# A tuned two-layer decoder kernel: a new time estimate in the builder's scheduler, and the order of steps that follows from it

## The chip, the cores and the metric

The kernel runs as one program on one core of one Trainium2 chip. The metric is device time in microseconds (us), the median of the runs shown. A core has a matrix engine (PE, with its weight loads as PEld), VectorE (DVE), ScalarE (ACT), GpSimd (POOL) and SyncE (SP, which only issues transfers here). Each engine runs its own list of instructions strictly in the order in which the program wrote them; semaphores make an instruction wait for results of other engines.

## The reference

Two layers over 512 tokens of width 1024, all in float32:

```
h = rms_norm(x);  proj = h @ w_in                 # q,k,v of branches A, B, C and three gates, 5376 columns
yA = MoBA attention (4 heads of 64, blocks of 256)
yB = sliding window 128, 8 query heads on 2 kv heads, with learned sinks
yC = differential attention (two softmax maps, P1 - lambda*P2), per-head norm
x  = x + (sum over b of sigmoid(gate_b) * (y_b @ w_p_b)) @ w_out
u  = causal_conv3(rms_norm(x) @ w_up);  x = x + (silu(u_gate) * u_val) @ w_down
```

q and k of every branch are RMS-normed and rotated before the scores.

## The kernel before

**Number format.** Each float32 operand is split in two parts, `whi`/`wlo` for weights and `H[0]`/`H[1]` for activations: the high part by a copy on ACT, the low part by a subtraction. A product is three matmuls (high·high, high·low, low·high). For a weight tile (128 rows x 1024) `w_prep` (L639) copies on ACT and subtracts either on DVE in one instruction or on POOL in four pieces of 256 columns. It takes POOL where `threads[1:] and est.clock["POOL"] <= est.clock["PE"] + POOL_LEAD`, that is while other work than the dense blocks is at hand; in blocks marked busy it always takes DVE.

**Dense blocks.** `dense` (L703) runs through a fixed list of blocks: per layer the steps of `ORDER` (layer 0) or `ORDER1` (layer 1), then two halves of `w_out`, eleven of `w_up`, two of `w_down`. A step `QC` is the q,k columns of branch C (512 columns, four weight tiles) and its v columns (256 columns, two tiles); `gC0` is half 0 of the gate of C (four tiles); `pC0` is half 0 of its output projection. A block walks its weight tiles; in each tile four output chunks get their matmuls, so that all four chunks end in the last tile. With `major=m` the last m tiles are taken chunk by chunk instead, and the chunks end further apart. Each chunk has a PSUM bank of four, which its evacuation frees.

**Norm ahead of the gates.** The steps before the first gate in an order are "raw": they use x times the gain without 1/rms, and the evacuation multiplies by 1/rms per token. From the first gate on, `H` must be normed. `renorm` (L583) does that for each of the eight 128-channel chunks k, once the last raw block is done with the chunk (`prog`): a multiplication on DVE, a copy on ACT, a subtraction on DVE. A later block's tile may start only when its chunks are in `normed`. Before the change the raw steps are QC and QA, and QA comes v first, then q,k.

**Attention.** `attention` starts when C's q,k block is done. Generators (threads) write its pieces: `prep` rotates and splits q and k for four token tiles (DVE, ACT, then PE transposes with PSUM copies in `move`), `score_thread` the scores, `soft` the masked maximum, exponentials and scaling, `trans_thread` the transposes of P, `spread` their split, `value_thread` the products with v, `gather` the output. The order is C, A, B, each in two halves.

**The planner.** The loop at the end of `trunk` chooses, while the program is built, which thread writes its next instructions. It keeps a simulated clock per engine in `Estimate` (L174): `cost` prices an instruction by engine, operation and size, `note` advances the clocks and records when a result is there, `ready` asks when a tensor can be read. A PE thread is taken if its inputs are ready by the PE clock plus `TOL`; otherwise the earliest. Threads of other engines are taken by priority (the `P_...` numbers and `RENORM`, smaller first) if they fit before that limit. The engines then execute this fixed order. So a wrong price puts a PE instruction ahead of data that is not there, and everything behind it on PE waits.

In `Estimate` before, a result is there 0.16 us (`SEM`) after its engine is free, for every engine and also for the same engine; a tensor's time is one number for all its pieces; DVE and POOL instructions that both read SBUF twice, or read it on POOL, wait for each other in the model.

Of the kernel before, what the change touches and what calls it, by code (L numbers as in the profile page):

```python
# [59 lines left out]
MAJ_OUT = 3  # L60
MAJ_DOWN = 0
MAJ_LAST = 3
FINE = 1
SPILL = 8

# [106 lines left out]


class Estimate:  # L174
    SEM = 0.16

    def __init__(self):
        self.clock = {"PE": 0.0, "ACT": 0.0, "DVE": 0.0, "POOL": 0.0, "SP": 0.3, "DGE": 0.0, "DMA": 0.0}
        self.table = None
        self.mode = None  # L180
        self.written = {}
        self.used = {}
        self.pred = {}
        self.rings = {}
        self.lock = LOCK
        self.port = {"DVE": deque(maxlen=24), "POOL": deque(maxlen=24)}

    def alloc(self, tag, bufs, t):
# [8 lines left out]
        i = len(ring) - bufs + n - 1  # L197
        return self.used.get(ring[i], 0.0) if i >= 0 else 0.0

    def ready(self, t):  # L200
        return self.written.get(t.tensor.name, 0.0) + self.SEM

    def cost(self, key, op, out, ins, kw, args):
        n = out.free_size()
        psum = any(x.space == bass.MemoryType.PSUM for x in (out, *ins))
        if key == "PE":
            move = op == "transpose"
            half = (out if move else ins[0]).dtype != F32
            was, self.mode = self.mode, (move, half)
            if move:  # L210
                return 0.072 if half else 0.109
            n = ins[1].free_size()
            if not half:
                return 2 * max(0.111, 8.4e-4 * n)
            return (0.0 if was in (None, self.mode) else 0.075) + max(0.111, 0.0133 + n / 2400)
        if key == "ACT":
            c = (0.053 if psum else 0.114) + 8.3e-4 * max([n] + [x.free_size() for x in ins])
# [9 lines left out]
            return c + (0.093 if "accum_out" in kw else 0.0)  # L227
        n = max([n] + [x.free_size() for x in ins])
        if key == "POOL":
            if kw.get("op") == OP.pow:  # L230
                return 0.3 + 0.165 * n
            return 0.172 + 2.03e-3 * n
        if op == "reciprocal":
            return 0.06 + 7.3e-3 * n
        if op in ("tensor_copy", "tensor_scalar", "memset") and not psum:
            return 0.065 + 6.0e-4 * n
        return (0.13 if op == "scalar_tensor_tensor" else 0.07) + 1.04e-3 * n

    def note(self, key, op, args, kw):
        aps = [x for x in list(args) + list(kw.values()) if isinstance(x, bass.AP)]  # L240
        out = kw.get("out", args[0] if args else None)
        if not isinstance(out, bass.AP):
            return
        outs = [out]
        if "accum_out" in kw and kw["accum_out"] is not None:
            outs.append(kw["accum_out"])
        if op == "tensor_tensor_reduce":
            outs.append(args[-1])
        ins = [x for x in aps if not any(x is o for o in outs)]
        t = self.clock[key]  # L250
        for x in ins:
            t = max(t, self.written.get(x.tensor.name, 0.0) + self.SEM)
        for o in outs:
            nm = o.tensor.name
            if key != "PE" and op != "dma_start":
                t = max(t, self.written.get(nm, 0.0) + (self.SEM if nm in self.written else 0.0))
            if nm[:2] in ("h0", "h1"):
                t = max(t, self.used.get(nm, 0.0) + self.SEM)
            if nm in self.pred:
                t = max(t, self.used.get(self.pred.pop(nm), 0.0) + self.SEM)  # L260
        if op == "dma_start":
            self.clock[key] = t + 0.06
            go = max(t + 0.1, self.clock["DGE"])
            self.clock["DGE"] = go + (0.475 if key == "SP" else 0.66)
            self.clock["DMA"] = max(self.clock["DMA"], go + 1.1) + 1.456 * out.size() / 131072
            end = self.clock["DMA"] + 0.75
        else:
            two = False
            if self.lock and key in ("DVE", "POOL"):
# [6 lines left out]
            if two:  # L276
                for s, e in self.port["POOL" if key == "DVE" else "DVE"]:
                    if s <= t < e:
                        t = e
            end = t + self.cost(key, op, out, ins, kw, args)  # L280
            self.clock[key] = end
            if two:
                gap = 0.05 if key == "POOL" else 0.0
                self.port[key].append((t + gap, end - gap))
        self.last = (t, end)
        for x in ins + outs:
            nm = x.tensor.name
            self.used[nm] = max(self.used.get(nm, 0.0), end)
        for o in outs:
            self.written[o.tensor.name] = max(self.written.get(o.tensor.name, 0.0), end)  # L290


class Thread:
# [37 lines left out]
def trunk(ctx: ExitStack, tc: tile.TileContext, out: bass.AP, a: dict):  # L331
    core = tc.nc
    est = Estimate()
# [1215 lines left out]
    def ready(y):  # L1549
        eng, needs, _ = y  # L1550
        r = 0.0
        for x in needs:
            if callable(x):
                x = x()
            r = max(r, x.when() if isinstance(x, Bufs) else est.alloc_ready(*x) if isinstance(x, tuple) else est.ready(x))
        return r

    def eng_clock(eng):
# [98 lines left out]
```

## Time and profile before

| | us |
|---|---|
| median of 3 runs | 1584.15 (1583.69 to 1584.84) |
| profiled execution, its own time | 1583.99 |
| its span, first to last instruction | 1582.1 |
| PE busy, PEld busy | 1544.0, 1281.9 |
| DVE, ACT, POOL busy | 1048.0, 800.8, 338.9 |

By time the span has these stretches: layer 0's QKV, gates, attention and projections from 0 to about 365, its `w_out` to 430, its `w_up` and `w_down` to about 794; layer 1's in the same order to about 1135, 1208 and the end. The granted PE clock is 0.999 of the upper level. A matmul's busy time covers its whole passage through the array, in which the next one has begun, so PE busy counts some waiting as work.

### The profile page before, as it was taken

Reading aid. Unit: us, or ns where it says so; the run is one execution under the profiler, and the core shown is the slowest. Engines: PE = TensorE matmul, PEld = TensorE weight load, DVE = VectorE, ACT = ScalarE, POOL = GpSimd, SP = SyncE. Lnnn points to the kernel's source line nnn. Section 1 sums busy time; section 2 is a strip of 40 time slices with the busy share of each in tenths; the row PEclk is TensorE's granted clock in tenths of the full one; section 3 lists DMA queues with packets and bytes.
Section 4 is the critical chain, followed back from the end, with each engine's and each line's share of the span. In section 5 each row is a group of like instructions: output and inputs, shape, how many; then the busy total and the mean of one; then the engine's idle time right before and its main releaser. Section 6 shows DMA issues by size and latency. Waiting matters only on the chain.

```text
span 1582.1 us, 21228 instructions
## 1 busy us (share of the span) xinstructions
PE 1544.0 (98%) x7584; PEld 1281.9 (81%) x7584; DVE 1048.0 (66%) x2211; ACT 800.8 (51%) x1566; POOL 338.9 (21%) x455
## 2 busy tenths in 40 slices
PE   8999999999999999999999999999999999999999
PEld 6977888877878888888888787888888788888887
DVE  4798878887576665543249887887776855665231
ACT  7566686764444444333146666766734544444210
POOL 3465443431010000000034564443300200000000
PEclk9999999999999999999999999999999999999999
DMA  5522523214223333333332224322242233223331
GB/s 176 154 68 79 173 68 94 80 54 135 90 83 107 89 98 107 107 98 127 95 114 69 66 79 160 107 67 61 73 159 88 72 106 107 80 86 101 120 120 53
DMA packets 115496, 157.22 MB, mean 99 GB/s; under 512 B 18880, under 2 KB 71104, under 8 KB 115392
## 3 DMA queue, kind: packets, MB, share of 16 engines
q1 hardware_dynamic: 102768, 153.19, 31.3%
q10 hardware_dynamic: 12624, 2.69, 0.9%
q8 instruction: 60, 0.98, 0.3%
q14 instruction: 44, 0.36, 0.1%
HBM read 144.84 MB, written 11.01 MB: 99 GB/s over the span
## 4 chain that ended last, share of the span: by engine, by line
PE 77%; DVE 14%; ACT 4%; DMA 2%; POOL 2%; issue 1%; SPq 0%; ACTq 0%; DVEq 0%; POOLq 0%
PE d L168 70%; PE tp L168 6%; DVE slot L168 5%; DVE temp L168 4%; ACT slot L168 2%; PE s L168 1%; DVE h L168 1%; ACT whi L168 1%; DVE s L168 1%; DMA raw<-in_w_up 1%; DVE wlo L168 1%; POOL rr L168 1%; DVE nb L168 1%; DMA slot<-in_c_cs 0%; ACT h L168 0%
## 5 line engine op out<-in xcount | busy, mean ns | idle before, releaser
L168 PE MATMUL d<-h,whi 128*128 128x512 f32 x2176 | 681.2, 394 | 4.0 <-DVE temp L168 2.7
L168 PEld LDWEIGHTS d<-h,whi 128*128 128x128 f32 x2176 | 398.6, 188 | 84.5 <-ACT temp L168 5.4
L168 PE MATMUL d<-h,wlo 128*128 128x512 f32 x1088 | 424.8, 390 | 0.0
L168 ACT CAST whi<-raw 128x1024 fp32r<-128x1024 f32 x246 | 256.2, 1052 | 280.2 <-PE d L168 136.3
L168 DVE TENSOR_TENSOR wlo<-raw,whi 128x1024 fp32r<-128x1024 f32 x175 | 213.5, 1233 | 257.9 <-ACT whi L168 257.5
L168 POOL TENSOR_TENSOR wlo<-raw,whi 128x256 fp32r<-128x256 f32 x284 | 225.2, 823 | 351.9 <-ACT whi L168 315.2
L168 PE MATMUL d<-slot,whi 128*128 128x512 f32 x864 | 267.0, 390 | 0.0
L168 PEld LDWEIGHTS d<-h,wlo 128*128 128x128 f32 x1088 | 204.2, 188 | 44.0
L168 PE MATMUL d<-whi,h 128*128 128x512 f32 (+1 forms) x768 | 205.9, 346 | 0.6 <-ACT h L168 0.6
L168 PEld LDWEIGHTS d<-slot,whi 128*128 128x128 f32 x864 | 161.1, 188 | 32.8
L168 DVE SCALAR_TENSOR_TENSOR temp<-d,packed,temp 128x511 f32<-128x511 f32 (+1 forms) x176 | 127.8, 747 | 63.4 <-ACT temp L168 60.3
L168 PE MATMUL d<-slot,wlo 128*128 128x512 f32 x432 | 168.2, 389 | 0.0
L168 PEld LDWEIGHTS d<-whi,h 128*128 128x128 f32 x768 | 134.8, 192 | 15.8 <-ACT h L168 1.0
L168 ACT CAST slot<-tp 128x256 fp32r<-128x256 f32 (+4 forms) x308 | 108.2, 379 | 70.8 <-PE tp L168 64.6
L168 PE MATMUL d<-wlo,h 128*128 128x256 f32 (+1 forms) x384 | 131.1, 341 | 0.2 <-DVE wlo L168 0.2
L168 ACT ACTIVATE temp<-d,packed 128x512 f32<-128x512 f32 x88 | 67.9, 773 | 86.1 <-PE d L168 79.4
L168 PE MATMUL d<-whi,slot 128*128 128x512 f32 x352 | 108.6, 389 | 0.0
L168 POOL TENSOR_TENSOR rn<-nvs,mhalf 128x4 f32<-128x4 f32 x3 | 3.0, 1008 | 482.4 <-DVE nvs L168 482.4
L168 DVE TENSOR_TENSOR slot<-slot,d 128x512 f32<-128x512 f32 x80 | 54.6, 685 | 73.9 <-PE d L168 71.2
L168 PEld LDWEIGHTS d<-slot,wlo 128*128 128x128 f32 x432 | 81.1, 188 | 17.0
L168 DVE TENSOR_TENSOR slot<-tp,slot 64x128 fp32r<-64x128 f32 (+4 forms) x180 | 76.0, 425 | 25.7 <-ACT slot L168 24.1
L168 ACT CAST slot<-temp 128x256 fp32r<-128x256 f32 (+2 forms) x140 | 58.1, 454 | 56.7 <-DVE temp L168 56.5
(113 smaller groups left out, 1784.8 us busy)
## 6 DMA issues: line engine op xcount, KB each, us to landing
raw<-in_w_up SPq DMA_DIRECT2D x176, 256.0 KB, 3.4
raw<-in_w_in SPq DMA_DIRECT2D x82, 512.0 KB, 3.7
raw<-in_w_down SPq DMA_DIRECT2D x44, 512.0 KB, 3.9
raw<-in_w_out SPq DMA_DIRECT2D x16, 512.0 KB, 4.6
x_spill<-slot SPq DMA_DIRECT2D x8, 512.0 KB, 3.9
b_parked<-slot SPq DMA_DIRECT2D x8, 512.0 KB, 5.3
slot<-b_parked SPq DMA_DIRECT2D x8, 512.0 KB, 5.8
raw<-in_w_pb SPq DMA_DIRECT2D x8, 512.0 KB, 3.7
```

Source lines behind the costliest of these rows:

```text
L168: r = f(*args, **kw)
```

## The change

All of it is in the planner and its constants; the arithmetic is the same. `cost` now returns two numbers, the time the engine is taken and a lag until the result is there (`LAG` by engine); `SEM` is by the engine that waits; a reader on the writing engine itself waits 0.01 us. Results are kept by piece of a tensor (`parts`, `box`, `when`). Several prices are new: the masked maximum on DVE (`tensor_tensor_reduce`), scaling with a per-token operand, the reciprocal, ACT and POOL base costs. At the shared port a DVE instruction that starts moves POOL's already planned pieces behind it (`push`). The constants and both orders are set anew:

```diff
-LOCK = True
-ORDER = ('QC', 'QA', 'gC0', 'QB', 'gC1', 'gA0', 'gA1', 'pC0', 'gB0', 'pC1', 'pA0', 'gB1', 'pA1', 'pB0', 'pB1')
+TURN = 0.075
+ORDER = ('QC', 'gC0', 'QA', 'gA0', 'QB', 'gA1', 'gC1', 'pC0', 'pC1', 'gB0', 'pA0', 'gB1', 'pA1', 'pB0', 'pB1')
-POOL_LEAD = 2.5
+POOL_LEAD = 1.0
-RENORM = 1.5
-EXTRA = ({'C': 0, 'A': 6, 'B': 0}, {'C': 13, 'A': 3, 'B': 35})
-GROOM = (0, 4)
-PRING = 3
-UNPARK = 6
-PTMAX = 6
+RENORM = 2.5
+EXTRA = ({'C': 4, 'A': 8, 'B': 8}, {'C': 6, 'A': 0, 'B': 30})
+GROOM = (1, 5)
+PRING = 4
+UNPARK = 7
+PTMAX = 5
-P_SCORE = 4.5
+P_SCORE = 3
-P_VALUE = 3.4
+P_VALUE = 1
-P_GATHER = 0.7
+P_GATHER = 0.15
-P_MOVE = 3.6
-P_PREP = 5
-TOL = 0.05
-COPY = 0.2
+P_MOVE = 0.1
+P_PREP = 4
+TOL = -0.05
+COPY = -0.5
-ORDER1 = ('QC', 'QA', 'gC0', 'QB', 'gC1', 'pC0', 'gA0', 'pC1', 'gB0', 'gA1', 'gB1', 'pA0', 'pA1', 'pB0', 'pB1')
+ORDER1 = ('QC', 'gC0', 'QA', 'QB', 'gC1', 'gA0', 'pC0', 'pC1', 'gA1', 'gB0', 'pA0', 'pA1', 'gB1', 'pB0', 'pB1')
-MAJ_OUT = 3
-MAJ_DOWN = 0
-MAJ_LAST = 3
+MAJ_OUT = 0
+MAJ_DOWN = 3
+MAJ_LAST = 4
...
 class Estimate:
-    SEM = 0.16
+    SEM = {"PE": 0.08, "ACT": 0.05, "DVE": 0.034, "POOL": 0.08, "SP": 0.1}
+    LAG = {"PE": 0.163, "ACT": 0.1, "DVE": 0.084, "POOL": 0.045}
...
+        if op == "tensor_tensor_reduce":
+            return 0.25 + 1.04e-3 * n, 0.0
         if op in ("tensor_copy", "tensor_scalar", "memset") and not psum:
-            return 0.065 + 6.0e-4 * n
-        return (0.13 if op == "scalar_tensor_tensor" else 0.07) + 1.04e-3 * n
+            return (0.13 if isinstance(args[2] if len(args) > 2 else None, bass.AP) else 0.075) + 5.2e-4 * n, lag
+        return (0.13 if op == "scalar_tensor_tensor" else 0.07) + 1.04e-3 * n, lag
...
+    def push(self, s, e):
+        for x in self.port["POOL"]:
+            if x[0] >= s - 1e-9 and x[0] < e:
+                d = e - x[0]
+                x[0] += d
+                x[1] += d
+                e = x[1]
...
```

In the new orders only QC stands before the first gate, so QC alone is raw, and QA and QB read the normed `H`.

## Rows read from the trace of the kernel before

**Rows 1.** Stretches: length, busy us of PE, PEld, DVE, ACT, POOL; clock, DMA.

```profile
40.00:365.00 325.00, 313.34 (x1756) 263.92 (x1755) 276.05 (x794) 214.21 (x523) 148.34 (x203) 0.99 0.32 95
460.00:803.00 343.00, 343.00 (x1517) 283.36 (x1516) 181.98 (x216) 131.15 (x165) 4.88 (x4) 1.00 0.33 103
840.00:1135.00 295.00, 285.69 (x1553) 236.44 (x1554) 245.80 (x728) 206.93 (x512) 135.67 (x184) 1.00 0.29 86
```

**Rows 2.** Chain of waits: start, us, what (one unbroken run of matmuls).

```profile
459.46 342.80 PE d L168 x1509
```

**Rows 3.** Timeline of PE: start, us, instruction (256 columns, then 512).

```profile
60.20 0.28 PE L168 MATMUL d<-wlo,h 128*128 128x256 f32 x1
...
60.56 0.28 PE L168 MATMUL d<-wlo,h 128*128 128x256 f32 x1
...
62.12 0.40 PE L168 MATMUL d<-wlo,h 128*128 128x512 f32 x1
```

**Rows 4.** Waits of PE, 40 to 125 us: total us, times, longest.

```profile
PE tp L168 <- DVE slot L168: 4.5, 4, 2.9
```

**Rows 5.** Waits of PE, 125 to 365 us.

```profile
PE tp L168 <- DVE slot L168: 5.4, 8, 1.3
```

**Rows 6.** Waits of PE, 832 to 912 us.

```profile
PE tp L168 <- DVE slot L168: 5.0, 8, 1.5
```

**Rows 7.** Waits of PE, 912 to 1135 us.

```profile
PE tp L168 <- DVE slot L168: 2.0, 6, 0.6
```

**Rows 8.** Timeline of PE: the longest of these, idle before and releaser in brackets.

```profile
85.02 0.30 PE L168 MATMUL tp<-identf,slot 128*128 128x128 f32 x1 [2.91 <-DVE slot L168]
```

**Rows 9.** Timeline of DVE just before it.

```profile
83.33 1.28 DVE L168 TENSOR_TENSOR h<-slot,h 128x512 fp32r<-128x512 f32 x2
```

**Rows 10.** DVE groups by shape: count, busy us, mean ns, idle before.

```profile
L168 DVE SCALAR_TENSOR_TENSOR slot<-slot,packed,slot 128x512 f32<-128x512 f32 x32 | 25.9, 849 | 5.9 <-ACT slot L168 5.9
...
L168 DVE TENSOR_TENSOR h<-slot,h 128x512 fp32r<-128x512 f32 x32 | 23.9, 773 | 5.7 <-ACT h L168 5.7
...
L168 DVE SCALAR_TENSOR_TENSOR h<-slot,packed,h 128x512 fp32r<-128x512 f32 x24 | 17.9, 746 | 0.0
```

**Rows 11.** Stretches of 10 us, columns as in rows 1.

```profile
50.00:60.00 10.00, 10.00 (x86) 10.00 (x85) 7.00 (x15) 3.73 (x7) 3.40 (x4) 1.00 0.70 214
60.00:70.00 10.00, 10.00 (x64) 8.51 (x63) 7.25 (x18) 6.50 (x17) 3.78 (x5) 1.00 0.31 98
...
815.00:825.00 10.00, 10.00 (x73) 9.41 (x72) 5.77 (x10) 6.42 (x10) 8.08 (x9) 1.00 0.35 79
825.00:835.00 10.00, 10.00 (x86) 10.00 (x85) 4.45 (x7) 3.78 (x6) 9.82 (x17) 1.00 0.25 68
```

**Rows 12.** Timeline of DVE: the rotation of two token tiles, one after the other.

```profile
53.15 0.82 DVE L168 TENSOR_TENSOR temp<-slot,slot 128x256 f32<-128x256 f32 x3
...
54.68 1.91 DVE L168 TENSOR_TENSOR temp<-slot,slot 128x256 f32<-128x256 f32 x3
```

**Rows 13.** Timeline of POOL beside the second of them.

```profile
54.67 3.40 POOL L168 TENSOR_TENSOR wlo<-raw,whi 128x256 fp32r<-128x256 f32 x4 [6.01 <-ACT whi L168]
```

**Rows 14.** DVE groups by shape: the masked row maximum and its second part.

```profile
L168 DVE CUSTOM_DVE_ANT_0 s<-s,mband 128x256 f32<-128x256 f32 x48 | 20.6, 429 | 6.8 <-PE s L168 3.8 <-ACT whi L168 1.1 <-ACT es L168 0.9
...
L168 DVE DVE_READ_ACCUMULATOR2_ANT mx<- 128x1 f32 x160 | 22.0, 137 | 0.2
```

**Rows 15.** POOL on the tile wlo alone: stretch, length, busy us (pieces).

```profile
40.00:365.00 325.00, 104.64 (x135) 0.99 0.32 95
```

**Rows 16.** DVE groups by shape: a whole weight tile, and the residual's add.

```profile
L168 DVE TENSOR_TENSOR wlo<-raw,whi 128x1024 fp32r<-128x1024 f32 x175 | 213.5, 1233 | 257.9 <-ACT whi L168 257.5
...
L168 DVE TENSOR_TENSOR slot<-slot,d 128x512 f32<-128x512 f32 x80 | 54.6, 685 | 73.9 <-PE d L168 71.2 <-ACT slot L168 2.3
```

**Rows 17.** Waits of PE, 1208 to 1255 us.

```profile
PE d L168 <- ACT h L168: 0.8, 1, 0.8
...
PE d L168 <- DVE h L168: 0.4, 1, 0.4
```

More of the change, by code (lines that the diff above doesn't have):

```diff
@@ L198, in alloc_ready, with ready, box, when @@
         return self.used.get(ring[i], 0.0) if i >= 0 else 0.0
-    def ready(self, t):
-        return self.written.get(t.tensor.name, 0.0) + self.SEM
+    def ready(self, t, key="PE"):
+        return self.written.get(t.tensor.name, 0.0) + self.SEM.get(key, 0.05)
+    @staticmethod
+    def box(x):
+        ap = x.ap
+        row = ap[0][0]
+        f = x.offset % row if row else x.offset
+        p = x.offset // row if row else 0
+        return p, p + ap[0][1], f, f + 1 + sum(abs(st) * (c - 1) for st, c in ap[1:])
+    def when(self, x, key):
+        parts = self.parts.get(x.tensor.name)
+        if not parts:
+            return 0.0
+        p0, p1, f0, f1 = self.box(x)
+        t = 0.0
+        for (a, b, c, d), k, e in parts:
+            if c < f1 and f0 < d:
+                t = max(t, e + (0.01 if k == key else self.SEM[key]))
+        return t
     def cost(self, key, op, out, ins, kw, args):
@@ L210, in cost @@
             if move:
-                return 0.072 if half else 0.109
+                return (0.072 if half else 0.109), lag
             n = ins[1].free_size()
             if not half:
-                return 2 * max(0.111, 8.4e-4 * n)
-            return (0.0 if was in (None, self.mode) else 0.075) + max(0.111, 0.0133 + n / 2400)
+                return 2 * max(0.111, 8.4e-4 * n), lag
+            return (0.0 if was in (None, self.mode) else TURN) + max(0.111, 0.0133 + n / 2400), lag
         if key == "ACT":
-            c = (0.053 if psum else 0.114) + 8.3e-4 * max([n] + [x.free_size() for x in ins])
+            c = (0.053 if psum else 0.1) + 8.3e-4 * max([n] + [x.free_size() for x in ins])
             for k in ("scale", "bias"):
@@ L249, in note @@
         ins = [x for x in aps if not any(x is o for o in outs)]
+        dma = op == "dma_start"
         t = self.clock[key]
         for x in ins:
-            t = max(t, self.written.get(x.tensor.name, 0.0) + self.SEM)
+            t = max(t, self.when(x, key))
         for o in outs:
             nm = o.tensor.name
-            if key != "PE" and op != "dma_start":
-                t = max(t, self.written.get(nm, 0.0) + (self.SEM if nm in self.written else 0.0))
+            if key != "PE" and not dma:
+                t = max(t, self.when(o, key))
             if nm[:2] in ("h0", "h1"):
-                t = max(t, self.used.get(nm, 0.0) + self.SEM)
+                t = max(t, self.used.get(nm, 0.0) + self.SEM[key])
             if nm in self.pred:
-                t = max(t, self.used.get(self.pred.pop(nm), 0.0) + self.SEM)
-        if op == "dma_start":
+                t = max(t, self.used.get(self.pred.pop(nm), 0.0) + self.SEM[key])
+        if dma:
             self.clock[key] = t + 0.06
@@ L268, in note @@
             two = False
-            if self.lock and key in ("DVE", "POOL"):
+            if key in ("DVE", "POOL"):
                 sb = [x.space != bass.MemoryType.PSUM for x in ins if x.free_size() > 1]
@@ L275, in note @@
                                           and out.space != bass.MemoryType.PSUM)
-            if two:
-                for s, e in self.port["POOL" if key == "DVE" else "DVE"]:
+            if two and key == "POOL":
+                for s, e in self.port["DVE"]:
                     if s <= t < e:
                         t = e
[L280 to L284, printed above, removed]
+            elif two:
+                for x in self.port["POOL"]:
+                    if x[0] <= t < x[1]:
+                        t = x[1]
+                        break
+            c, lag = self.cost(key, op, out, ins, kw, args)
+            self.clock[key] = t + c
+            end = t + c + lag
+            if two and key == "POOL":
+                self.port[key].append([t, t + c, out.tensor.name, self.box(out)])
+            elif two:
+                self.port[key].append((t, t + c))
+                self.push(t, t + c)
         self.last = (t, end)
@@ L289, in note @@
         for o in outs:
-            self.written[o.tensor.name] = max(self.written.get(o.tensor.name, 0.0), end)
+            nm = o.tensor.name
+            self.written[nm] = max(self.written.get(nm, 0.0), end)
+            p0, p1, f0, f1 = box = self.box(o)
+            keep = [y for y in self.parts.get(nm, ()) if not (p0 <= y[0][0] and y[0][1] <= p1 and f0 <= y[0][2] and y[0][3] <= f1)]
+            keep.append((box, key, end))
+            self.parts[nm] = keep
 class Thread:
@@ L1554, in ready @@
                 x = x()
-            r = max(r, x.when() if isinstance(x, Bufs) else est.alloc_ready(*x) if isinstance(x, tuple) else est.ready(x))
+            r = max(r, x.when() if isinstance(x, Bufs) else est.alloc_ready(*x) if isinstance(x, tuple) else est.ready(x, eng))
         return r
```

15 lines of the change are left out of this document (10 added, 5 removed).

## The prediction

> **What bounds the kernel now.** I read the stretches first. They give the busy time of each engine between two times, and the reader is to compare PE's with the length. In layer 0's up and down projections PE is busy for all of 343.0 us; in the two attention stretches it is busy for 313.3 of 325 and 285.7 of 295 us, 11.7 and 9.3 us short [rows 1]. In the attention stretches DVE is busy 85% and 83%, in the dense one 53%. So the dense part is matmul for matmul, and nothing of an order can shorten it; what an order can win lies where DVE is nearly full.
>
> Next the chain of waits, for the pace of PE: 1509 matmuls of 512 columns took 342.8 us, so one starts every 0.227 us [rows 2]. With 256 columns three start in 0.36 us, 0.12 us each [rows 3]. A matmul of 512 columns is shown as 0.40 us long, 0.17 us more than the pace; when PE stands, the first 0.17 us are covered by the last matmul and don't show as idle.
>
> Then the list of waits of PE, stretch by stretch: what it waited for, in total, how often. DVE is the first entry in all four: 4.5 us in 4 waits, 5.4 in 8, 5.0 in 8, 2.0 in 6 [rows 4 to 7]. With 0.17 us for each these are 5.2, 6.8, 6.4 and 3.0 us, 21.4 together.
>
> The last view is the timeline at the longest wait. PE stood 2.91 us at a transpose of P, for a result of DVE [rows 8]; DVE had in front of it two subtractions of `renorm` [rows 9]. Nobody on PE needed these two yet. That is the form of the loss: the planner held DVE for less loaded than it was, and put work of no haste ahead of work that PE stood for.
>
> **The change part by part.** All durations are of the profiled execution, 1583.99 us with a span of 1582.1; its distance to the median of 1584.15 is nothing here. The arithmetic stays, so PE's matmuls stay: every gain must come out of waits.
>
> *(a) The gates move ahead of QA, so `renorm` moves ahead too.* Before, QC and QA were raw, and `H` was normed while QA ran. Now it must be normed from QC's v block on. `renorm` costs DVE eight times 0.849 + 0.773, that is 13.0 us per layer [rows 10], and this work leaves the stretches where DVE is fullest (70 to 120 us, 850 to 900). Where it goes, DVE has room: 3.0 and 2.75 us free between 50 and 70, that is 5.75; 4.2 and 5.55 free between 815 and 835, that is 9.8 [rows 11]. So 44% and 75% of it find an idle DVE, and the rest pushes C's rotation back by as much as it gave. I let PE's waits for DVE in these stretches fall by the same shares: 0.44 x 5.2 + 0.75 x 6.4 = 7.1 us. Both ends: all 11.6 us go, or, if `renorm` is late, the waits grow (rival S). The cover that is lost is QA: 96 matmuls of 0.227 and 96 of 0.12, 33.3 us, stood between the end of QC and the first reader of a normed `H`. What is left is the second tile of QC's v, 48 x 0.12 = 5.8 us, and then 24 x 0.227 = 5.45 us for each pair of chunks. A pair costs DVE 3.24 us, so it holds if little comes between.
>
> On the port that DVE and POOL share: with POOL idle three multiplications of the rotation took 0.82 us; with POOL on its pieces of `wlo` the same three took 1.91 [rows 12, 13]. The means of `renorm` hold some of this already: its multiplication takes 0.849 us, the like instruction that runs in the dense part, where POOL is nearly idle, 0.746 [rows 10]; that is 0.1 us for each. [...]
>
> *(b) The prices, the priorities and the rest of the order.* The masked maximum of 256 columns was priced 0.07 + 0.00104 x 256 = 0.34 us; it takes 0.429 and a second part of 0.137, 0.57 together, 160 times [rows 14]. The new price is 0.52. So the old clock of DVE ran ahead by some 0.23 x 80 = 18 us per layer, in the very chain (scores, maximum, exponential, transposes) at whose end PE waits. With a right clock the planner puts the transpose of P later and a dense matmul first. At stake are the waits for DVE outside (a), 6.8 + 3.0 = 9.8 us. I take a third, 3.3 us: DVE's work is not less, so part of the waits only moves. Ends: all 9.8 gained, or as much lost, since some ten priorities and the room rules (`PRING`, `PTMAX`, `EXTRA`, `UNPARK`) change with it and no row shows the new order. The DMAs that move with these steps are the weights of QA and of the gates, six and four tiles that SP issues in the order of use, two ahead as before, and B's five stores and loads, which go with QB. PE's waits are led by DVE in every stretch [rows 4 to 7], so I give them nothing; a late tile would cost some microseconds once.
>
> *(c) `POOL_LEAD` 2.5 to 1.0.* POOL did 135 pieces, 34 tiles, of layer 0's stretch [rows 15]. A tile that goes to DVE costs it 1.233 us [rows 16] and spares it about 1.09 (1.91 - 0.82) where a rotation lay beside it. A tile takes POOL 3.4 us [rows 13] and PE at least 5.45, so POOL's clock is rarely over 1 us ahead and few tiles go. Taken at nothing; half the tiles would be 17 x 0.14 = 2.4 to 17 x 1.23 = 21 us of DVE per layer, in stretches with 49 us free.
>
> *(d) `MAJ_OUT` 3 to 0.* Four chunks of the second half of `w_out` ended 18 x 0.227 = 4.1 us apart, now 6 x 0.227 = 1.4. Each gives DVE an add into the residual (0.685), a split (0.746) and an add of the squares (about the first again): 2.1 us [rows 10, 16]. The last was done 2.1 us after the last matmul; now 4 x 2.1 - 3 x 1.4 = 4.2 or a little more: 2.3 us later, and with it 1/rms and `renorm`. In layer 1 PE already waits for `H` in the second `w_up` block, 0.8 and 0.4 us [rows 17], so I add 2.3 us there and none in layer 0 (ends: 0 and 4.6). In exchange the weight buffers come free tile by tile, which I value at nothing.
>
> *(e)* `MAJ_DOWN` 0 to 3 makes `H` of layer 1 earlier, where PE waits for nothing; `MAJ_LAST` 3 to 4 leaves the last chunk's matmuls, add and store as they are; QA's evacuation without the factor is a little shorter on ACT, off the path. Nothing for each.
>
> Sum: -7.1 - 3.3 + 2.3 = -8.1 us; 1584.0 - 8.1 = 1575.9, so **1576 us**.
>
> **The rivals.** *G, the new clock takes nearly all waits for DVE:* 1584 - 21.4 + 2.3 = 1565 us. For it: each wait is short, and dense matmuls were at hand behind it. Against: DVE stays over 80% busy, and its results come no sooner. [...]
>
> *N, the waits only change their place,* or the new estimate doesn't order better: 1581 to 1587 us. For it: DVE's total hardly changes. Against: (a) uses idle time of DVE that was lost before.
>
> *S, the first gate waits for `renorm`,* slower. Place: the four tiles of gC0 in each layer. In 5.45 us DVE owes 3.24 for `renorm` and two token tiles of C's rotation. These three multiplications take 2 x 0.82 when POOL is idle, 4.9 us in all, and PE doesn't wait; they take 2 x 1.91 when POOL subtracts beside them, 7.1 us, and PE loses 1.6 us a tile, 6.4 a layer, 12.9 in both. It decides from 1.1 us for the three on. Then (a) is a loss: 1584 + 12.9 - 3.3 + 2.3 = 1596 us, half as much where POOL's pieces lie beside half of them, 1589. For it: POOL was busy 3.4 to 9.8 of 10 us there [rows 11]. Against: `renorm` is still ahead of C's rotation in priority (2.5 to 4).
>
> **How the numbers follow.** The forecast (1570 to 1581 us) has 0.45, G 0.16, N 0.17, S 0.22. A change under 0.2% (3.2 us) can't be told from none here. So faster 0.61, same 0.17, slower 0.22. The range goes from a little below G, 1562, to the middle of S, 1593; about 0.13 is left out.
>
> **What would show it.** (a): `renorm` instructions near 45 to 70 and 815 to 845 us, DVE there fuller, and the 2.9 us wait gone; (b): the lists of waits of both attention stretches shorter, DVE first no more; (d): a longer wait for `H` some 25 us after layer 1's `w_out`. The prediction is wrong if gC0's first matmuls wait for `H` by more than 3 us a layer (S), if the four totals for DVE stay above 15 us (N), or if PE's busy share in the dense stretch changes at all.

## The result, and the profile after

The changed kernel takes 1597.45 us (median of 4 runs, 1595.81 to 1599.16) against 1584.49 of the kernel before on the same chip: ratio 1.0085, interval [1.0073, 1.0098]. It is 13 us slower; the prediction said 8 us faster, and its range ended at 1593. The profiled execution took 1599.16 us with a span of 1597.4.

The stretches of [rows 1] again (length, busy us of PE, PEld, DVE, ACT, POOL; clock, DMA):

```profile
40.00:365.00 325.00, 313.67 (x1746) 263.26 (x1744) 269.24 (x790) 214.40 (x524) 136.52 (x188) 0.99 0.31 95
460.00:803.00 343.00, 341.69 (x1505) 281.90 (x1505) 183.21 (x220) 132.16 (x168) 4.88 (x4) 1.00 0.32 100
840.00:1135.00 295.00, 281.55 (x1556) 234.16 (x1557) 253.90 (x749) 195.56 (x493) 124.60 (x167) 0.99 0.28 84
```

The dense stretch lies 3 to 5 us later in the changed kernel, so the same window begins and ends in other work. The 1.3 us by which PE is short there are two waits, now at 460.3 and 462.9 us, that lay at 456.8 and 459.5 us before, outside the window. Inside the stretch the chain of waits shows the same pace as [rows 2], 335.14 / 1476 = 0.227 us:

```profile
462.94 335.14 PE d L168 x1476
```

So the loss is in the attention stretches, as any gain would have been. Taken from the timeline of PE: layer 0 up to its first `w_up` matmul 430.0 us before, 434.5 after; layer 1 from its first matmul to its `w_up` 413.8 before, 426.9 after; the two stretches of up and down projections 364.6 and 369.8 before, 363.4 and 368.7 after. These are the two profiled executions, which lie 15.2 us apart where the medians lie 13 apart.

The waits of PE, in the four stretches of [rows 4 to 7] in turn (total us, times, longest):

```profile
PE d L168 <- ACT h L168: 2.0, 1, 2.0
PE d L168 <- DVE h L168: 1.3, 1, 1.3
PE tp L168 <- DVE slot L168: 1.0, 2, 0.8
...
PE s L168 <- ACT slot L168: 2.7, 5, 1.0
PE tp L168 <- ACT slot L168: 1.5, 1, 1.5
PE tp L168 <- DVE slot L168: 1.0, 5, 0.3
...
PE tp L168 <- DVE slot L168: 3.7, 5, 1.2
PE d L168 <- ACT h L168: 2.2, 2, 2.0
PE d L168 <- DVE h L168: 1.2, 1, 1.2
...
PE tp L168 <- DVE slot L168: 5.2, 8, 1.2
PE s L168 <- ACT slot L168: 2.6, 4, 1.2
```

The waits for DVE's slots, on which the forecast rested, did fall in total, from 16.9 to 10.9 us: 4.5, 5.4, 5.0, 2.0 before, now 1.0, 1.0, 3.7, 5.2. Three fell and the last rose. In their place stand waits for `h` (3.3 and 3.4 us) and for ACT. The waits for `h` are rival S's place, the first gate. PE's timeline in layer 0 (idle before and releaser in brackets), from the end of QC:

```profile
49.99 0.28 PE L168 MATMUL d<-whi,h 128*128 128x256 f32 x1
52.28 0.49 PE L168 MATMUL d<-h,whi 128*128 128x512 f32 x1 [2.02 <-ACT h L168]
54.10 0.80 PE L168 MATMUL d<-h,whi 128*128 128x512 f32 x1 [1.32 <-DVE h L168]
```

And in layer 1, where QC's last matmul starts at 834.63:

```profile
836.92 0.49 PE L168 MATMUL d<-h,whi 128*128 128x512 f32 x1 [2.02 <-ACT h L168]
838.59 0.80 PE L168 MATMUL d<-h,whi 128*128 128x512 f32 x1 [1.17 <-DVE h L168]
```

Why it is late is on DVE's timeline in layer 0. The first multiplications of `renorm` (49.85) stand behind evacuations of C's v, each of which waits, through ACT's half of the evacuation, for QC's own matmuls; so in this list `renorm` does not start before QC ends, although DVE has idle time there:

```profile
46.50 0.48 DVE L168 SCALAR_TENSOR_TENSOR slot<-d,rn,slot 128x256 fp32r<-128x256 f32 x1 [0.34 <-ACT slot L168]
47.94 0.48 DVE L168 SCALAR_TENSOR_TENSOR slot<-d,rn,slot 128x256 fp32r<-128x256 f32 x1 [0.96 <-ACT slot L168]
49.45 0.48 DVE L168 SCALAR_TENSOR_TENSOR slot<-d,rn,slot 128x256 fp32r<-128x256 f32 x1 [1.03 <-ACT slot L168]
49.85 2.07 DVE L168 SCALAR_TENSOR_TENSOR slot<-slot,packed,slot 128x512 f32<-128x512 f32 x3
```

The wait has a second price. In stretches of 5 us the granted clock (before the DMA columns) falls behind it:

```profile
50.00:55.00 5.00, 1.66 (x6) 1.05 (x5) 5.00 (x8) 2.96 (x5) 0.00 (x0) 0.83 0.64 200
55.00:60.00 5.00, 5.00 (x13) 3.84 (x13) 4.96 (x11) 3.84 (x6) 1.09 (x1) 0.50 0.53 197
60.00:65.00 5.00, 5.00 (x24) 4.12 (x23) 4.96 (x9) 1.55 (x3) 3.68 (x4) 0.99 0.05 6
```

From 55 to 60 PE is "busy" throughout, but 13 matmul records stand where the next 5 us have 24: at 0.50 one takes 0.43 us (two in the 0.86 us from 55.12 to 55.98), at 1.00 0.227 [rows 2]. That is another 2.5 us or so (11 x 0.227), and the same is seen at 840 to 845 (0.50, 11 records). So S's place costs about 6 us a layer, near the 6.4 that the prediction gave it. But that is not what decides, as the runs show.

### The profile page after: what moved, and what is told of

It reads as the page before. It is cut to its first block, busy times and chain, and to the rows that moved or that the text cites. A ratio compares the mean times of both kernels' runs of the same rounds, so it can differ in the third digit from the quotient of the medians.

```text
span 1597.4 us, 21202 instructions
## 1 busy us (share of the span) xinstructions
PE 1549.9 (97%) x7584; PEld 1284.4 (80%) x7584; DVE 1049.2 (66%) x2228; ACT 797.0 (50%) x1556; POOL 318.9 (20%) x427
## 4 chain that ended last, share of the span: by engine, by line
PE 78%; DVE 14%; ACT 5%; issue 1%; DMA 1%; POOL 0%; SPq 0%; POOLq 0%; ACTq 0%; DVEq 0%
PE d L168 71%; DVE slot L168 6%; PE tp L168 5%; DVE temp L168 4%; ACT slot L168 3%; PE s L168 2%; DVE s L168 1%; ACT whi L168 1%; DVE nb L168 1%; DVE wlo L168 1%; DMA raw<-in_w_in 1%; ACT L168 0%; ACT h L168 0%; DVE h L168 0%; DVE mx L168 0%
## 5 line engine op out<-in xcount | busy, mean ns | idle before, releaser
L168 DVE TENSOR_TENSOR wlo<-raw,whi 128x1024 fp32r<-128x1024 f32 x182 | 222.3, 1233 | 266.4 <-ACT whi L168 265.9
L168 POOL TENSOR_TENSOR wlo<-raw,whi 128x256 fp32r<-128x256 f32 x256 | 204.2, 828 | 372.6 <-ACT whi L168 351.9
```

Of the source, the lines that this page charges most:

```text
L168: r = f(*args, **kw)
```

## Experiments

Each diff is against the kernel named. Lengths of a layer are those above, up to its first `w_up` matmul.

### Which part of the change: estimate, orders, constants

The change has three parts that can be set apart: the class `Estimate` and its callers, the two orders, and the constants. All eight combinations exist with the two kernels and six runs.

**e1**, after with the old orders; **e2**, after with the old constants; **e3**, after with both old, that is the new estimate alone:

```diff
 # e1
-ORDER = ('QC', 'gC0', 'QA', 'gA0', ...
+ORDER = ('QC', 'QA', 'gC0', 'QB', ...
 # and ORDER1; e2: POOL_LEAD ... MAJ_LAST as before; e3: both
```

> The changed kernel with ORDER and ORDER1 of the kernel before; the new estimate and all other constants stay. Theory S (the new place of the first gate and of the later steps costs the 13 us): back to 1584 to 1587 us, no wait of PE for h between 45 and 60 and around 836 us, no stretch at a granted clock of 0.5. Theory E (the new estimate orders the pieces worse): 1594 to 1599. Theory C (the other constants do it): 1594 to 1599.

> The changed kernel with all other constants of the kernel before (POOL_LEAD, RENORM, EXTRA, GROOM, PRING, UNPARK, PTMAX, the P_ numbers, TOL, COPY, MAJ_*); new estimate and new orders stay. Theory C: back to 1584 to 1588. Theories S and E: 1594 to 1602; under S the waits for h before the first gate stay, 3 us a layer.

> The kernel before with the new estimate alone; orders and constants are the old ones. Theory E: 1592 or more, with more waits of PE for DVE in both attention stretches. Theories S and C: 1582 to 1588.

**e5**, before with the new orders; **e6**, before with the new constants; **e7**, before with both:

```diff
 # e5: ORDER and ORDER1 as after; e6: the constants; e7: both
-    SEM = {"PE": 0.08, ...
+    SEM = 0.16
```

> The kernel before with ORDER and ORDER1 of the change, old estimate and old constants. If the new orders cost by themselves (with the new estimate and the new constants they cost 9.6 us): 1590 to 1597, with PE waiting for h before the first gate. If orders, constants and estimate only fit or don't fit each other: no telling from the parts; anything from 1584 to 1615, with the losses at other places than in the changed kernel.

> The kernel before with the other constants of the change, old estimate and old orders. If the constants cost by themselves: over 1590. If the new constants are good ones (with the new estimate and the old orders they gave 28 us): below 1584. If they fit the new estimate only: 1588 to 1610.

> The changed kernel with the old estimate: new orders, new constants. If the new estimate costs by itself (alone it cost 31.6 us): below 1590. If orders and constants were fitted to the new estimate, the old one does worse with them: over 1600.

Measured, median us (ratio to before, interval; the kernel before 1583.3 to 1584.1 beside them):

| | old orders | new orders |
|---|---|---|
| old estimate, old constants | 1584.1 | e5 1588.5 [1.0018, 1.0042] |
| old estimate, new constants | e6 1605.0 [1.012, 1.015] | e7 1609.9 [1.0152, 1.0186] |
| new estimate, old constants | e3 1615.8 [1.0183, 1.0213] | e2 1593.8 [1.0043, 1.0076] |
| new estimate, new constants | e1 1587.9 [1.0014, 1.0034] | after 1597.5 [1.0073, 1.0098] |

Estimate and constants are a pair: with the old orders each alone costs 21 to 32 us, the two together 4. And the orders cost 4 to 10 us in three of the four rows. No part has a price of its own. The traces show the same by layer (us, as above):

| | layer 0, old `ORDER` | new `ORDER` | layer 1, old `ORDER1` | new `ORDER1` |
|---|---|---|---|---|
| old estimate and constants | 430.0 | 426.0 (e9) | 413.8 | 423.8 (e5) |
| new estimate and constants | 429.2 (e1) | 434.5 (after) | 419.3 (e1) | 426.9 (after) |

In layer 0 the new `ORDER` gains 4.0 us with the old pair and loses 5.3 with the new one.

### The gate ahead of QA, by layer

**e4**, after with QA ahead of gC0 again in both orders, which takes away S's wait:

```diff
-ORDER = ('QC', 'gC0', 'QA', 'gA0', 'QB', ...
+ORDER = ('QC', 'QA', 'gC0', 'gA0', 'QB', ...
```

> The changed kernel with one thing put back: QA stands before gC0 again in both layers (QC, QA, gC0, ...), all else as changed. Theory S in its narrow form (the gate waits for renorm, with the slower matmuls after it): 1585 to 1589, and no wait for h before the first gate. If the loss lies in the later steps of layer 1 (1000 to 1160 us, where the changed kernel waits 5.1 us for DVE and 2.3 for ACT): 1594 or more.

1598.2 [1.0077, 1.0107], no better than after. The waits for `h` at the first gate are gone from its list, and the layers take 433.5 and 426.2 us, after 434.5 and 426.9: what the gate gave back was lost elsewhere. In layer 1 it is the end of QA, where PE waits 3.7, 1.7 and 3.6 us for pieces of attention between 873 and 886 us. Taking S's wait away doesn't bring the time back. It also puts a price on step (a) in the changed kernel: after is 0.7 us faster than e4, which the intervals can't tell from nothing.

**e9**, before with the new `ORDER` in layer 0 and nothing else; **e10**, after with the old `ORDER1` in layer 1:

```diff
 # e9, against before
-ORDER = ('QC', 'QA', 'gC0', 'QB', 'gC1', 'gA0', ...
+ORDER = ('QC', 'gC0', 'QA', 'gA0', 'QB', 'gA1', ...
 # e10, against after: ORDER1 = ('QC', 'QA', 'gC0', 'QB', 'gC1', 'pC0', ...
```

> The kernel before with the new ORDER in layer 0 alone; ORDER1, estimate and constants are the old ones. In the run with both new orders layer 0 reached its up projection at 425.3 us and not 430.0, and layer 1 took 10 us longer from its first matmul to its up projection. If that loss belongs to ORDER1, this kernel keeps the first and not the second: 1578 to 1581, faster than the kernel before. If layer 1 is late because of what layer 0 leaves behind: 1586 to 1590.

> The changed kernel with the old ORDER1; ORDER, estimate and constants as changed. If the new ORDER1 costs layer 1 about 8 us with these constants too: 1588 to 1591, and layer 1 takes 419 us (not 427) from its first matmul to its up projection. If both orders must be old for it: 1594 or more.

e9: **1578.63 us** (1577.70 to 1579.11), ratio 0.9963 [0.9948, 0.9978]. It beats both kernels. Layer 0 takes 426.0 us, 4.0 less than before, though PE waits for `h` there as in after. The waits of PE in e9, 40 to 125 us and 125 to 365:

```profile
PE d L168 <- ACT h L168: 3.2, 1, 3.2
PE d L168 <- DVE h L168: 0.5, 1, 0.5
PE tp L168 <- DVE slot L168: 0.3, 1, 0.3
...
PE tp L168 <- DVE slot L168: 3.0, 5, 1.1
```

Against [rows 4, 5] the waits for DVE's slots fall from 9.9 to 3.3 us; the gate takes 3.7 of that back, and the lower clock behind it (0.50 from 55 to 60 us) more. That is seen when every 512 columns are counted at 0.227 us and every 256 at 0.12 and the remainder is called lost (us lost in stretches of 30 us of layer 0). The count is rough: the price of the smaller matmuls, and records that the trace lacks, move an entry by up to about 1 us.

```
        30-60  60-90  90-120  ...  330-360  360-390
before    0.0    6.4     1.3           3.0      1.9
e9        7.2    1.5     0.6           0.9      0.1
```

Up to 120 us the gate takes back all that `renorm`'s move gives, and 1.6 us more; most of the gain of layer 0 stands at the end of attention, in waits for its last pieces. That the later steps of `ORDER` cover these is an inference; they were not run alone.

e10: 1591.94 [1.0034, 1.0064]. Layer 1 takes 419.7 us instead of 426.9. So the new `ORDER1` costs 5.5 us with the new estimate and constants (7 in the traces), and 9.9 with the old ones (e5 less e9). One account of the whole, which goes by e9 and e10: new `ORDER` -5.4 (e9), estimate with constants +13.3 (e10 less e9), `ORDER1` +5.5 (after less e10); together +13.4. By e1 the same sum is split otherwise: estimate with constants +3.8, new `ORDER` +4.1 (e10 less e1), `ORDER1` +5.5.

**e13** and **e14** split `ORDER1` on the base of e9: the first has the new head, the second the new tail.

```diff
 # e13
-ORDER1 = ('QC', 'QA', 'gC0', 'QB', 'gC1', 'pC0', 'gA0', ...
+ORDER1 = ('QC', 'gC0', 'QA', 'QB', 'gC1', 'pC0', 'gA0', ...
 # e14: 'QC', 'QA', 'gC0', 'QB', 'gC1', then 'gA0', 'pC0', 'pC1', 'gA1', 'gB0', 'pA0', 'pA1', 'gB1', ...
```

> The kernel before with the new ORDER in layer 0, and in layer 1 the old ORDER1 with one step moved: gC0 goes ahead of QA, the rest as before. It splits the 10 us by which the whole new ORDER1 made layer 1 longer (1588.5 against 1578.6 us). Head theory: the first gate, whose four tiles now follow QC, waits for renorm with PE's clock halved (5.8 us more in its 30 us, in the run with both old partners), and this isn't given back; about 1585 us, layer 1 up to its w_up 418 to 421 us against 413.2. Tail theory: the loss comes from gA0 ahead of pC0 and pC1 ahead of gA1 and from gB0 to gB1 with two pA blocks between, at which gates are used up early and the later pieces of attention have no dense block beside them; then this run is at 1577 to 1581 us. As layer 0 gained 4 us with the same step moved, I hold half of the loss, some 3 to 6 us, for the head.

> The kernel before with the new ORDER in layer 0, and in layer 1 the old head (QC, QA, gC0, QB, gC1) with the new tail (gA0, pC0, pC1, gA1, gB0, pA0, pA1, gB1, pB0, pB1). Tail theory: the waits behind 180 us of layer 1 come with it (2.9 us for a slot from DVE, 2.5 us near the end), 1584 to 1588 us, layer 1 up to its w_up 419 to 423 us. Head theory: 1577 to 1581 us. If the losses of this run and of its twin add up to about 10 us, the two parts are independent; if the sum is far from it, the planner's list reacts to each change as a whole and no step has a price of its own.

e13: 1587.68 [1.0016, 1.0040]; e14: 1586.12 [1.0005, 1.0023]. That is 9.1 and 7.5 us over e9, while head and tail together cost 9.9 (e5). So neither part is the cause by itself, and the two prices don't add: the list reacts to each change as a whole. What the head does can be placed by the same count of lost time (stretches from layer 1's first matmul):

```
        30-60  60-90  90-120  ...  180-210  210-240  240-270
e9        3.6    2.5     6.6           2.1      1.1      1.3
e13       9.4    5.7     2.1           6.0      2.3      4.6
```

From 90 to 120 it gains 4.5 us, nearly the 4.8 of step (a); the first gate takes 5.8 and its neighbour 3.2, and from 180 to 270 another 8.4 go, in pieces of attention that come later than the list had them. The profiled execution of e13 took 1592.43 us, 4.8 above the median of its six, so not all of these losses are in the 9.1. At the gate, e13's timeline of PE:

```profile
829.51 1.69 PE L168 MATMUL d<-h,whi 128*128 128x512 f32 x2 [4.34 <-ACT h L168]
```

### The clock behind the wait

**e8** fills the wait: eighteen matmuls of 512 columns, whose results nobody reads, ahead of gC0 in both layers of after, and the planner counts them. **e12** is the same with the planner not told, so that the rest of the list stays as in after. **e18** does it in layer 0 alone on the base of e9.

```diff
+            if br == "C" and half == 0:
+                blocks[-1].fill = 18
...
+                        if b.fill and i == 0 and c == 0:
+                            whi = W[b.t0][0]
+                            for _ in range(b.fill):
+                                core.tensor.matmul(ps[0], whi[:, :128], whi[:, :512], start=True, stop=True)
 # this is e12; e8 has nc.tensor, which the planner counts; e18 adds `and l == 0`
```

> The changed kernel with 18 matmuls of 512 columns (4.1 us) that nobody reads put on PE ahead of the first matmul of gC0 in each layer; they read the weight tile alone, so they run while PE would wait for h. If the slower granted clock behind these waits (0.5 from 52 to 59 and from 837 to 844 us) comes of PE standing still, it stays at 1.0 and the kernel gains what the slow matmuls cost, 4 to 5 us for both layers: 1592 to 1594. If the clock falls for another reason, or the renorm work sets the pace there anyway: 1597 to 1599.

> As the run with 18 idle matmuls ahead of gC0, but the planner isn't told of them, so that the order of all other instructions is that of the changed kernel. If the clock falls because PE stands still: granted clock 1.0 from 52 to 60 and from 837 to 845 us, layer 0's up projection at 431 to 432 and not 434.5, layer 1's part shorter by 2 to 3 us: 1591 to 1593. If the clock costs nothing: 1597 to 1598.

> The kernel before with the new ORDER in layer 0 alone (1578.6 us, the fastest so far), and ahead of gC0 in layer 0 eighteen matmuls of 512 columns whose results nobody reads, in place of PE's standing. They fill the 3.2 and 0.5 us for which PE waits for the normed H near 50 us there, after which its granted clock is 0.82 and 0.50 in the next 10 us. Clock theory: the wait stays lost, what the halved clock costs (2.4 us in layer 0 of the filled kernel after) comes back: 1575 to 1577 us. Rival: the matmuls delay the first gate by more than the wait, or what is saved comes back as a wait for a piece of attention a little later, as in layer 1 of the filled kernel after, which gained nothing: 1578 to 1580 us.

e8: 1595.17 [1.0060, 1.0090]; e12: 1595.57 [1.0054, 1.0088]; e18: 1578.18 [0.9950, 0.9977], where e9 has [0.9948, 0.9978]. The clock stays up in e12, in the stretches of after above:

```profile
50.00:55.00 5.00, 5.00 (x26) 4.24 (x26) 4.99 (x8) 2.98 (x5) 0.00 (x0) 1.00 0.58 222
55.00:60.00 5.00, 5.00 (x24) 4.14 (x23) 5.00 (x10) 3.42 (x6) 0.52 (x1) 1.00 0.73 210
```

That matmuls without a purpose keep the clock up at the gate is shown: it fell there in every trace in which PE stood at layer 0's first gate (to 0.50 from 55 to 60 us in after and e9), and in none of e8, e12 and e18 (1.00 in the same 5 us of e12 and e18). It is worth little. e12 reaches `w_up` 2.4 us earlier than after in layer 0 (432.1) and takes 0.4 less in layer 1 (426.5), where 2 to 3 were expected. And of the 2.4 us only 0.8 are there when PE comes to its last long wait of layer 0's attention, 2.70 us for a slot of DVE, which is the same in both lists. The other 1.6 come behind that wait, because the clock fell there in after (0.73) and not in e12 (1.00). After:

```profile
365.00:370.00 5.00, 3.83 (x11) 3.06 (x12) 2.35 (x8) 2.26 (x6) 2.81 (x4) 0.73 0.08 12
```

e12:

```profile
365.00:370.00 5.00, 4.59 (x20) 3.86 (x21) 2.69 (x7) 2.10 (x5) 2.63 (x4) 1.00 0.20 48
```

In e18 the fill is worth nothing: the rival there was right.

### `MAJ_OUT` alone

**e11**:

```diff
-MAJ_OUT = 3
+MAJ_OUT = 0
```

> The kernel before with MAJ_OUT = 0 alone. By my prediction's step (d) the waits for h in layer 1's second up block grow by 2.3 us: 1586 to 1587. By the traces (up and down projections 1.2 and 1.1 us shorter in the changed kernel) it is a gain: 1581 to 1583.

1583.75, ratio 0.9994 [0.9985, 1.0004]. No change. Step (d) had +2.3; in after the waits for `H` in `w_up` are 1.3 us together, against 1.2 in [rows 17].

### The masked maximum's price alone, and the dense stock

**e15** puts one price right in the kernel before; this is the price of step (b) by itself, with (b)'s priorities and order left old. **e16** is e10 with `renorm` ahead again.

```diff
 # e15, against before
+        if op == "tensor_tensor_reduce":
+            return 0.25 + 1.04e-3 * n
 # e16, against e10
-RENORM = 2.5
+RENORM = 1.5
```

> The kernel before with one price put right: the masked maximum on DVE (tensor_tensor_reduce) 0.25 + 0.00104 n, 0.52 us for 256 columns, in place of 0.34. This is step (b) of the prediction by itself. By the prediction PE's waits for DVE outside of the renorm stretches fall by a third, 3.3 us: 1580 to 1581 us. The rival: the old constants were set for the old prices, so a right price alone gives a list that is no better and likely worse, as with the whole new estimate alone (1615.8 us, 31.7 us slower): 1584 to 1595 us.

> The kernel after with the old ORDER1 (1591.9 us) and one constant more put back: RENORM 1.5 in place of 2.5. In that kernel layer 1 has one wait of 10 us at the end of QA, where gC0 starts. Theory: renorm stands behind P_MOVE 0.1, P_GATHER 0.15 and P_VALUE 1 and comes late, so the first gate waits even after QA; with 1.5 it is still behind P_VALUE 1 and P_MOVE, but ahead of the splits (1.9) and squashes (2.1): the wait falls from 10 us to under 3, and the time to 1583 to 1587 us. Rival: what is late isn't renorm's place among the priorities but its inputs or DVE's load (x times gain, 1/rms, POOL's power), then the wait stays at 8 to 11 us and the time at 1589 to 1595 us.

e15: 1611.66 [1.0163, 1.0197], 28 us **slower** with a price that agrees with [rows 14] to 0.05 us; its layers are 14.9 and 12.3 us longer. The rival had the direction, but not the size. e16: 1606.64 [1.0128, 1.0159]; PE's waits of 10 us ahead of the first gate of layer 1 become 4.4, and 19 us are lost 100 us later, so that neither of its two forecasts came true. In e15 the same 30 us of layer 1 lose 19 us, and the end of layer 0's attention 26. These are the busy times of the dense tile `d` alone, first from layer 1's first matmul over 176 us, then over the 30 us behind it (length, PE, PEld, DVE, ACT; clock, DMA). The kernel before:

```profile
794.60:970.60 176.00, 142.84 (x721) 113.54 (x719) 6.93 (x15) 23.08 (x47) 1.00 0.34 102
970.60:1000.60 30.00, 21.73 (x86) 15.04 (x84) 2.65 (x4) 2.35 (x4) 1.00 0.19 53
```

e15:

```profile
809.30:985.30 176.00, 154.02 (x757) 121.76 (x756) 7.67 (x16) 22.88 (x47) 0.99 0.32 101
985.30:1015.30 30.00, 3.54 (x13) 2.05 (x12) 0.00 (x0) 1.76 (x3) 0.75 0.17 55
```

e16:

```profile
796.80:972.80 176.00, 154.72 (x765) 122.57 (x764) 6.91 (x14) 23.95 (x49) 0.99 0.33 103
972.80:1002.80 30.00, 1.18 (x6) 0.62 (x4) 1.38 (x2) 0.00 (x0) 0.72 0.22 78
```

Over 176 us e15 and e16 did 11 to 12 us more of dense work on PE; over the next 30 they had next to none, at a clock of 0.75 and 0.72. What there is of PE's work then is attention, piece by piece, each waiting for DVE and ACT. PE's timeline of e15:

```profile
994.22 0.46 PE L168 MATMUL tp<-identr,slot 128*128 128x128 f32 x4
1001.46 1.84 PE L168 MATMUL tp<-onesr,slot 128*128 128x2 f32 x8 [6.78 <-DVE slot L168]
```

and DVE's and ACT's beside it. DVE itself waits for a cast on ACT (999.47), which stands behind a table load and a run of activations, four of them the sigmoids of gates:

```profile
1000.12 0.69 DVE L168 TENSOR_TENSOR slot<-slot,slot 128x512 fp32r<-128x512 f32 x1 [4.79 <-ACT slot L168]
...
993.73 1.28 ACT L168 ACT_TABLE_LOAD   x1
995.03 4.41 ACT L168 ACTIVATE slot<-slot 128x1024 f32<-128x1024 f32 x5
```

The kernel before has such a load and four sigmoids (3.90 us) at 992.7 us as well, with dense work on PE beside them: PE does not wait from 990 to 1001 us there.

The reading is this. The gates are a stock: a fixed number of dense matmuls that need nothing from attention, while pC0 behind them needs its output. A later forecast of DVE makes the planner put a dense matmul into each short gap and hold the pieces of attention back. The gaps shrink, the stock is gone early, and then PE has nothing to lay beside the pieces. e3 (the new estimate with the old constants) shows it too: 153.95 and then 1.63 us.

**e17** takes the pieces earlier again, with e15's price:

```diff
-TOL = 0.05
+TOL = 0.60
```

> The kernel of e15 (the kernel before with the masked maximum priced right, 1611.7 us) with TOL 0.60 in place of 0.05, so that a piece of attention is taken on PE up to 0.6 us ahead of its forecast time, rather than a dense matmul. Stock theory: with the later forecast of DVE the planner filled every short wait with a dense matmul, the gates were used up early, and near 995 us (and 355 us) PE had some 60 pieces of attention in a row with nothing dense between them, at half clock: 19 and 26 us lost there. In the list of e17 no run of pieces as long as that is left (in e15 there are two, of 61 and 75 matmuls; in the kernel before none). So the two stalls go, short waits come back before them (some 5 to 10 us), and the time is 1584 to 1593 us. Rival: the loss is not the lack of dense work but DVE's load or the chain of attention itself, which a few more or fewer dense matmuls between don't hasten; then the time stays at 1603 to 1615 us, with longer waits in other places.

1636.82 [1.0319, 1.0347]: a clear miss in the time, by 44 us. The stall did go, as its theory said: of e17, the same two stretches:

```profile
817.60:993.60 176.00, 123.73 (x584) 95.95 (x584) 4.60 (x10) 19.18 (x34) 0.97 0.24 69
993.60:1023.60 30.00, 15.47 (x98) 13.61 (x97) 1.70 (x4) 4.10 (x15) 0.94 0.32 99
```

Now 19 us less dense work than before in the first stretch, and PE stands in waits for ACT's and DVE's slots instead (15.2 us, the longest 5.6; the kernel before has 6.6, the longest 1.5); this cost more than the stall (layers of 452.5 and 445.3 us; e15 444.9 and 426.1). So the stall comes and goes with the dense work: it is there in e3, e15 and e16, where the stock is gone early, and not in e17, where it is kept. That the time lost in e15 could be had back with another `TOL` is not shown: 0.6 us lost more than it gained, and a value between was not tried. So e17 also leaves its rival open, that the pace of attention itself sets the time.

## Why the prediction was wrong

**Step (b) failed, in sign.** It read the waits for DVE, saw that a dense matmul was at hand behind each, and took a right price for a gain of 3.3 us. The dense matmul is not free: it is taken from a stock that a later piece needs. The old price, 0.23 us too low for each maximum by [rows 14], had the pieces of attention early, and with its 16.9 us of waits PE kept dense work to the end of attention. e15 measures the price alone, in the old list, at +28 us; the prediction's end for (b) was 9.8 us lost, so even its bounds were too near. In the change itself the constants go with the prices, and no stall as big is left; but estimate and constants together still cost 3.8 us with the old orders (e1) and 13.3 with the new `ORDER` (e10 less e9). The rest of the order, which (b) also held, costs 7.5 us in layer 1 (e14 less e9).

Where these 13.3 us lie: 6.5 in layer 1, most of it one place in e10 (and in e1 and e4 too), at the end of QA, where the list puts pieces of attention before the gate. PE's timeline there:

```profile
874.04 0.28 PE L168 MATMUL tp<-slot,slot 128*128 128x256 f32 x1
878.17 0.50 PE L168 MATMUL tp<-slot,slot 128*128 128x256 f32 x2 [3.85 <-DVE slot L168]
880.66 1.24 PE L168 MATMUL s<-slot,slot 128*128 128x384 f32 x2 [1.99 <-ACT slot L168]
...
886.26 0.69 PE L168 MATMUL s<-slot,slot 128*128 128x384 f32 x1 [3.56 <-ACT slot L168]
```

In layer 0 it is 8.8 us, while the two stretches of up and down projections give 2.1 back. Of the 8.8 the count of lost time shows 6.2 from 330 to 390 us, at the end of attention: a wait for a late slot of DVE, as this line of after has it, and the clock behind it (0.73 from 365 to 370 us). The rest stays open, as does which of the prices and constants do it.

```profile
366.17 1.16 PE L168 MATMUL tp<-slot,slot 128*128 128x512 f32 x4 [2.70 <-DVE slot L168]
```

**Step (a) failed too: the waits went, the gain did not come with them.** Forecast were 7.1 us; in the changed kernel the step is worth 0.7 (after against e4). The waits fell where it said so: for DVE from 4.5 to 1.0 us in layer 0 and from 5.0 to 3.7 in layer 1, and in e13 the lost time of layer 1 falls by 4.5 us from 90 to 120 us, against a forecast of 4.8. But the gate took it back at once, by 7.2 us in layer 0 (e9), by 5.8 and 3.2 in layer 1 (e13). The cover that the step counted on, 5.8 us of QC's second v tile, was not there: `renorm` first ran at 49.85 us, and QC's last matmul starts at 49.99. The 4.0 us that layer 0 gains under the new `ORDER` look like (a)'s 2.3, but most of them stand at the end of attention (e9's count); no run split that order. The reading of idle time in DVE between 50 and 70 us missed the order of DVE's list: `renorm` (49.85 us) stands in it behind QC's last evacuations (to 49.45) and does not use the idle time ahead of them (0.34, 0.96 and 1.03 us).

**S had its place and size, but not its mechanism.** I priced it by POOL's pieces beside the rotation; in after POOL did nothing from 50 to 55 us. The sign that the prediction set for S, over 3 us of waits for `H` a layer, was there (3.3 and 3.4). But that S's 1596 us lies near the measured 1597.5 is luck: without the wait the kernel takes 1598.2 (e4). The subtraction and the multiplication of `renorm` in after, both layers:

```profile
L168 DVE TENSOR_TENSOR h<-slot,h 128x512 fp32r<-128x512 f32 x32 | 27.6, 892 | 0.9 <-ACT h L168 0.7
...
L168 DVE SCALAR_TENSOR_TENSOR slot<-slot,packed,slot 128x512 f32<-128x512 f32 x32 | 23.8, 790 | 6.8 <-ACT slot L168 6.8
```

51.4 us together, 49.8 in [rows 10]: 1.6 us more of DVE's time in both layers. The prediction priced POOL's part by these means, and they hide two sizes. Alone, a subtraction takes 0.68 us and a multiplication 0.75; beside a piece of POOL's `wlo`, held up, either takes about 1.22. Of the 64 instructions 15 are of the long kind in after and 12 were before, so most of the moved `renorm` met no POOL at all. Where it did, in layer 1, six subtractions took 6.95 us:

```profile
845.73 6.95 DVE L168 TENSOR_TENSOR h<-slot,h 128x512 fp32r<-128x512 f32 x6
845.63 7.64 POOL L168 TENSOR_TENSOR wlo<-raw,whi 128x256 fp32r<-128x256 f32 x7 [5.63 <-ACT whi L168]
```

What a hold-up adds here is about 0.5 us (1.22 less 0.68 or 0.75), less than the 0.85 us of a whole piece (3.40 / 4, [rows 13]). Why DVE is held up is not shown: the shared port that the prediction names stands in the planner's model (`port`), and the traces have the lengths alone.

**N and G** are out by their numbers: the four totals fell to 10.9 us, under the 15 that stood for N, and the time rose all the same. A list of waits that gets shorter does not show a gain, if other rows and the clock aren't added up. N's second clause, that the new estimate doesn't order better, is what e1 and e10 show, at more than its price.

**(c)** held: DVE did 182 whole tiles of `wlo` instead of 175. **(d)**, +2.3 in the sum, measured nothing (e11). **(e)** held, but each up and down stretch became 1.1 to 1.2 us shorter.

## What to carry to other kernels

A list scheduler's wrong price and its tuned thresholds are one thing: correcting the price alone can cost far more than the waits that it seems to cause. Before counting a wait as room, ask what independent work would fill it and what that work covers later; a fixed stock of fill only moves the wait, and in e15 and e16 the stall at its end cost the clock too (0.75 and 0.72). Try an order's change one layer at a time, and with the old constants as well: layer 0's half alone wins 0.37% there (e9) and loses with the new ones.

## What the runs showed of the hardware

In the nine traces in which PE stands 2.6 to 3.8 us at layer 0's first gate (after, e2, e5, e7, e9, e10, e13, e14, e16) the granted clock fell behind it (to 0.50 from 55 to 60 us in after and e9); in the three with the stand filled (e8, e12, e18) it stayed at 1.00.

Elsewhere the same wait goes either way. The wait of 2.70 us at the end of layer 0's attention was followed by a lower clock in after (0.73 from 365 to 370 us) and e10, and not in e12 (1.00 there) and e8. The 2.91 us of [rows 8] did not lower it in this trace of the kernel before, 85 to 90 us:

```profile
85.00:90.00 5.00, 4.54 (x24) 3.73 (x25) 4.90 (x16) 3.09 (x7) 3.19 (x4) 1.00 0.00 0
```

In e11, whose order is the same there and whose wait is 2.90 us, it did:

```profile
85.00:90.00 5.00, 5.00 (x18) 3.98 (x19) 4.90 (x16) 1.83 (x4) 3.30 (x4) 0.71 0.00 0
```

And a shorter one did in the kernel before: 1.33 us at 148.4, with a clock of 0.66 from 150 to 155. So length alone does not tell the two outcomes apart; what does is not shown.
